# Scores of two heads on 64 rows of the array each, three products a head, in an encoder's attention

## The chip, the cores and the metric

The kernel runs on one core of one Trainium2 chip. The core has TensorE (PE in the profile; its weight loads are listed apart as PEld), VectorE (DVE), ScalarE (ACT), GpSimd (POOL) and SyncE (SP), and 16 DMA engines. The metric is the device time of one execution in microseconds (us).

## The reference

Two layers of an encoder on 512 tokens of width 1024, in float32. Each layer is a feed-forward half-step, a mixer with three attention branches, and a second feed-forward half-step. The mixer, cut to what matters here:

```python
u = rmsnorm(h, mix_pre_g[l])
qa, ka, va, qb, kb, vb, qc, kc, vc, gl = jnp.split(u @ w_in[l], split_at, axis=-1)
oa = neighbourhood_attention(...)    # A: 8 heads of 64, 2-D window and a bias
ob = sliding_window_attention(...)   # B: 8 query heads on 2 key heads, rotary, |i-j| <= 128, a sink logit
oc = differential_attention(...)     # C: 4 heads with two softmax maps each, rotary, dense
yb = jnp.einsum('bsnc,ncd->bsnd', branches, w_branch[l])
merged = jnp.sum(gates * yb, axis=2)
h = h + rmsnorm(merged @ w_out[l], mix_post_g[l])
```

Scores are q.k over a head width of 64, for all three branches.

## The kernel before

Activations lie transposed: channels on the 128 partitions, 512 tokens along the free dimension. A block of 128 channels of q or k therefore holds two heads of 64, the one on partitions 0 to 63 and the other on 64 to 127. To get float32 accuracy from TensorE's one-pass float32r, each operand is split into a high part (rounded) and a low part (the rest); `split` does it with one ACT copy and one DVE subtraction. A dense product of a 128x128 weight block with 512 tokens is three matmuls (high.high, high.low, low.high; `mm3`, lines 298 to 300), and one block of projected channels (`dense1`) is 24 of them, accumulated in one PSUM bank with the tag "mm". "Dense" below means these matmuls.

PSUM has eight banks: four "mm", three "at" (scores, transposes and transposed operands), one "o".

Scores before: `stacks` writes, for each head, by DMA, a tile of 128 rows whose upper half is the high part and whose lower half is the low part (tile "st"), and for keys also the swapped one (tile "sw"). With rows stacked so, the product q.k with all four pairs of parts is two matmuls over 128 rows (lines 1337 and 1338 in A and B, 1475 and 1476 in C). A stack costs two transfers of 64 rows, on the SP queue. The queue also carries the rotary shuffles ("sh") and the bias tables of branch A ("braw").

A and B are worked off in units of two heads ("aa0" to "aa3", "ab0" to "ab3"), the heads one after the other in `softmax_pv`: for each of four query blocks of 128, scores over a window of 256 or 384 keys; DVE adds the bias and takes the row's extreme in one instruction (line 1341); ACT takes the exponent with the row sum (1350); DVE the reciprocal (1355) and the scaling (1357). Then, for each of four key blocks: PE transposes of the probabilities (1365), a split (324 on ACT, 325 on DVE), and two matmuls with the values into bank "o" (1368, 1369); at the end ACT copies half of "o" (1371) and DVE adds the halves (1372). C does the same with the whole 512 keys and two maps a head (lines 1475 to 1503).

The order in which the units are written is the table `ORDER`: "qa0" makes q, k, v of a unit, "aa0" attends, "ga", "ya" and so on are gates and branch products (dense work). This order is a priority only. The framework's scheduler sets the order of instructions on each engine: it takes written order as priority and moves an instruction forward where an earlier written one still waits for an operand or a buffer by its own estimate. Buffers come from tagged pools with a fixed number of slots (`ABUFS`, `PBUFS`), and a tile waits until a slot of its tag is free. What the scheduler has ordered is then fixed: each engine works through its own list in order.

Of the kernel before, what the change touches and what calls it, by code (L numbers as in the profile page):

```python
# [34 lines left out]
KP = KF - 2 * KS  # L35
HOLD_OUT = ("g", "g", "g", "g", "g", "tx", "tx", "pt")
# [73 lines left out]
def encoder_kernel(ctx: ExitStack, tc: tile.TileContext, order, xT, wts, cols, rows, rpb, consts, tables, out):  # L110
# [10 lines left out]
    ABUFS = {"f": {"t": 4, "x": 10}, "m": {"t": 5, "h": 4, "rr": 2, "tx": 5, "st": 16, "g": 10, "s": 2, "pt": 4}}  # L121
# [27 lines left out]
    def f(t):  # L149
        return t.bitcast(F32)  # L150
# [1148 lines left out]
    def stacks(x, both):  # L1299
        hi, lo = split(x, "tx")  # L1300
        res = []
        for s in range(2):
            own = slice(64 * s, 64 * s + 64)
            st = big("st", F32R, name="st")
            nc.sync.dma_start(f(st)[0:64], f(hi)[own])
            nc.sync.dma_start(f(st)[64:128], f(lo)[own])
            sw = None
            if both:
                sw = big("st", F32R, name="sw")
                nc.sync.dma_start(f(sw)[0:64], f(lo)[own])  # L1310
                nc.sync.dma_start(f(sw)[64:128], f(hi)[own])
            res.append((st, sw))
        return res

# [14 lines left out]
    def softmax_pv(sq, sk, vof, bias, scale, sink, odst, oview):  # L1329
        ss, nmx = [], small("nmx")  # L1330
        sall, at = big("s", shape=(P, NT * T), name="s"), 0
        for i in range(NT):
            j0, j1 = window(i)
            n = (j1 - j0) * P
            sp = bank("at")[:, :n]
            qs = sq[0][:, i * P : (i + 1) * P]
            PE.matmul(sp, qs, sk[0][:, j0 * P : j1 * P], start=True, stop=False)
            PE.matmul(sp, qs, sk[1][:, j0 * P : j1 * P], start=False, stop=True)
            s = sall[:, at : at + n]
            at += n  # L1340
            V.tensor_tensor_reduce(
                out=s, in0=sp, in1=bias(i), scale=-1.0, scalar=3e38, op0=ALU.add, op1=ALU.min,
                accum_out=nmx[:, i : i + 1],
            )
            ss.append(s)
# [41 lines left out]
    def mixer(l, op, first):  # L1387
# [42 lines left out]
        def qkv_a(q, k, v):  # L1430
            sq, sk = stacks(plain(q, True, 0.125), False), stacks(plain(k, True), True)
            return sq, sk, turn(plain(v, True), 2)
# [3 lines left out]
        def attn_a(p, sq, sk, vof):  # L1436
            o = big("t", name="o")
            for s in range(2):
                softmax_pv(
                    sq[s], sk[s], lambda j, s=s: vof(j, s), biases(2 * p + s), 1.0, None,  # L1440
                    perm(o[64 * s : 64 * s + 64, :]), natural,
                )
# [7 lines left out]
        def attn_b(p, sq, skb, vofb):  # L1450
            o = big("t", name="o")
            for s in range(2):
                hd = 2 * p + s
                kv = hd // 4
                softmax_pv(
                    sq[s], skb[kv], lambda j, kv=kv: vofb(j, kv), bias_b, 0.125,
                    (sink[:, l, hd : hd + 1], nsink[:, l, hd : hd + 1]),
                    o[64 * s : 64 * s + 64, :], lambda ap: ap,
                )
            OT["b", p] = split(o, "g")  # L1460
# [3 lines left out]
        def attn_c(sq, sk, v):  # L1464
            vh, vl = v
            aa = []
            sall = big("s", shape=(P, NT * T), name="s")
            for i in range(NT):
# [3 lines left out]
                for s in range(2):  # L1472
# [8 lines left out]
                    e = big("tx", name="e") if s else sall[:, i * T : (i + 1) * T]  # L1481
# [54 lines left out]
        def qkv_b(c):  # L1536
            return stacks(rope(dense1(w, l, c, X), cosR, sinR), c == KB)

        def qkv_c(hd):
            sq = stacks(rope(dense1(w, l, QC + hd, X), cosR, sinR), False)  # L1540
            sk = stacks(rope(dense1(w, l, KC + hd, X), cosR, sinR), True)
            return sq, sk, turn(plain(dense1(w, l, VC + hd, X), False), 1)
# [40 lines left out]
        for u in ORDER.split():  # L1583
# [4 lines left out]
        hN = [big("s", shape=(P, 2, 2, T), name="h") for _ in range(2)]  # L1588
# [5 lines left out]
            l, "mix_post_g", (1.0, 1.0), ("ffn2_pre_g", l), gains, lambda tb, n: hN[tb // 2][:, tb % 2, n, :],  # L1594
# [129 lines left out]
```

## Time and profile before

| | us |
|---|---|
| three runs | 2440.2, 2442.27 (median), 2444.3 |
| the profiled execution, its own time | 2441.57 |
| its span in the profile | 2439.8 |

| engine | busy us | share |
|---|---|---|
| PE | 2404.1 | 99% |
| PEld | 2111.5 | 87% |
| DVE | 1797.8 | 74% |
| ACT | 1347.5 | 55% |
| POOL | 192.1 | 8% |

Busy times of PE are of overlapping matmuls with modelled ends: one takes 0.39 us where the next starts 0.23 us after it. So the cost of a matmul in a row of others is read from the distance between starts. The two mixers' attention lies between about 389 and 770 us and between about 1597 and 1995 us of the span. Line numbers in the profile of before are those of the functions above.

### The profile page before, as it was taken

Reading aid. Unit: us, or ns where it says so; the run is one execution under the profiler, and the core shown is the slowest. Engines: PE = TensorE matmul, PEld = TensorE weight load, DVE = VectorE, ACT = ScalarE, POOL = GpSimd, SP = SyncE. Lnnn points to the kernel's source line nnn. Section 1 sums busy time; section 2 is a strip of 40 time slices with the busy share of each in tenths; the row PEclk is TensorE's granted clock in tenths of the full one; section 3 lists DMA queues with packets and bytes.
Section 4 is the critical chain, followed back from the end, with each engine's and each line's share of the span. In section 5 each row is a group of like instructions: output and inputs, shape, how many; then the busy total and the mean of one; then the engine's idle time right before and its main releaser. Section 6 shows DMA issues by size and latency. Waiting matters only on the chain. (4 is left out here: it accounts for less than half of the span.)

```text
span 2439.8 us, 37786 instructions
## 1 busy us (share of the span) xinstructions
PE 2404.1 (99%) x14298; PEld 2111.5 (87%) x14298; DVE 1797.8 (74%) x2943; ACT 1347.5 (55%) x2471; POOL 192.1 (8%) x192
## 2 busy tenths in 40 slices
PE   9999999999999999999999999999999999999998
PEld 8999888888877889998899998888877778899987
DVE  8887976857667467888878878776676764788786
ACT  6555655646555365555655555555465554555553
POOL 0111000000111100110001110000001111011100
PEclk9999999999999999999999999999999999999999
DMA  5566536445442334654435565373454333356642
GB/s 170 162 163 182 169 132 175 116 113 149 111 131 95 111 105 132 169 154 162 170 95 157 156 173 190 116 183 106 113 143 124 110 103 121 96 147 165 184 144 87
DMA packets 119190, 340.59 MB, mean 140 GB/s; under 512 B 15968, under 2 KB 22752, under 8 KB 118496
## 3 DMA queue, kind: packets, MB, share of 16 engines
q1 hardware_dynamic: 91344, 224.85, 29.9%
q10 hardware_dynamic: 22032, 79.78, 10.9%
q0 software_dynamic: 5632, 33.56, 6.8%
q8 instruction: 112, 1.84, 0.3%
q14 instruction: 70, 0.57, 0.1%
HBM read 285.16 MB, written 48.23 MB: 137 GB/s over the span
## 5 line engine op out<-in xcount | busy, mean ns | idle before, releaser
L298 PE MATMUL mm<-X,w 128*128 128x512 f32 (+1 forms) x1044 | 397.1, 380 | 2.2 <-ACT w L199 1.7
L299 PE MATMUL mm<-X,w 128*128 128x512 f32 (+1 forms) x1044 | 396.8, 380 | 0.7 <-DVE X L522 0.7
L300 PE MATMUL mm<-X,w 128*128 128x512 f32 (+1 forms) x1044 | 396.1, 380 | 0.0
L200 DVE TENSOR_TENSOR w<-wr,w 128x512 fp32r<-128x512 f32 x360 | 255.3, 714 | 168.2 <-ACT w L199 167.0
L199 ACT ACTIVATE w<-wr 128x512 fp32r<-128x512 f32 x360 | 223.4, 627 | 226.6 <-PE mm L300 184.3
L842 PE MATMUL mm<-ht,l 128*128 128x256 f32 x1120 | 316.5, 283 | 0.0
L842 PE MATMUL mm<-ht,h 128*128 128x256 f32 x1120 | 316.3, 282 | 0.0
L842 PE MATMUL mm<-lt,h 128*128 128x256 f32 x1120 | 315.6, 282 | 0.0
L298 PEld LDWEIGHTS mm<-X,w 128*128 128x128 f32 x1044 | 197.4, 189 | 34.0 <-ACT w L199 1.9
L299 PEld LDWEIGHTS mm<-X,w 128*128 128x128 f32 x1044 | 197.2, 189 | 32.2 <-DVE X L522 1.1
L300 PEld LDWEIGHTS mm<-X,w 128*128 128x128 f32 x1044 | 197.1, 189 | 31.4
L842 PEld LDWEIGHTS mm<-ht,l 128*128 128x128 f32 x1120 | 213.1, 190 | 0.0
L842 PEld LDWEIGHTS mm<-ht,h 128*128 128x128 f32 x1120 | 213.0, 190 | 0.0
L842 PEld LDWEIGHTS mm<-lt,h 128*128 128x128 f32 x1120 | 212.7, 190 | 0.0
L1082 PE MATMUL mm<-wh,f 128*128 128x512 f32 x640 | 200.3, 391 | 0.0
L842 PE MATMUL mm<-X,h 128*128 128x256 f32 x1120 | 200.3, 279 | 0.0
L842 PEld LDWEIGHTS mm<-X,h 128*128 128x128 f32 x1120 | 171.2, 189 | 0.3
L842 PE MATMUL mm<-X,l 128*128 128x256 f32 x560 | 155.4, 278 | 0.0
L1082 PEld LDWEIGHTS mm<-wh,f 128*128 128x128 f32 x640 | 120.3, 188 | 26.9
L702 DVE TENSOR_TENSOR l<-wr,h 128x1024 fp32r<-128x1024 f32 x70 | 85.7, 1224 | 78.5 <-PE mm L842 78.5
L1082 PE MATMUL mm<-wl,f 128*128 128x512 f32 x320 | 126.6, 396 | 3.1 <-DVE wl L959 3.1
L324 ACT ACTIVATE hi<-at 128x256 fp32r<-128x256 f32 (+2 forms) x168 | 77.2, 474 | 73.4 <-PE at L1365 37.9
(366 smaller groups left out, 5458.5 us busy)
## 6 DMA issues: line engine op xcount, KB each, us to landing
wr<-in_wts_dram SPq DMA_DIRECT2D x223, 512.0 KB, 4.7
wr<-in_wts_dram ACTq DMA_DIRECT2D x152, 512.0 KB, 3.6
sum<-in_wts_dram POOLq DMA_DIRECT2D x64, 512.0 KB, 5.5
st<-hi SPq DMA_DIRECT2D x84, 128.0 KB, 2.5
st<-lo SPq DMA_DIRECT2D x84, 128.0 KB, 3.4
ap<-in_wts_dram SPq DMA_DIRECT2D x20, 512.0 KB, 6.7
a<-kept SPq DMA_DIRECT2D x32, 256.0 KB, 5.9
ap<-sum SPq DMA_DIRECT2D x16, 512.0 KB, 4.7
```

The lines of the kernel that those rows point to most:

```text
L199: A.activation(hi, raw, AF.Copy)
L200: V.tensor_tensor(out=lo, in0=raw, in1=f(hi), op=ALU.subtract)
L298: PE.matmul(acc, w[0], x[0], start=start, stop=False)
L299: PE.matmul(acc, w[0], x[1], start=False, stop=False)
L300: PE.matmul(acc, w[1], x[0], start=False, stop=stop)
L324: A.activation(hi, src, AF.Copy)
L702: V.tensor_tensor(out=W[g]["l1"], in0=raws[g][0], in1=f(W[g]["h1"]), op=ALU.subtract)
L842: PE.matmul(acc, ws[i], xs[j], start=start and k == n == 0, stop=stop and k == HK - 1 and n == 2, skip_group_check=True,)
L1082: PE.matmul(acc, x[i], w[j], start=start and n == 0, stop=stop and n == 2, skip_group_check=True)
```

## The change

`stacks` goes. `parts` splits q and k in place, with no transfer; only the two key heads of B are copied by DMA, so that each lies on both halves of the partitions (`twice`). `scores` makes the scores of both heads of a unit (in C: of both maps of a head) for one query block: one bank "at" for the head on rows 0 to 63, one bank "mm" for the head on rows 64 to 127, and three matmuls of 64 rows a head, written alternately. `attend` makes the scores of both heads over all query blocks first, and then calls `softmax_pv` for the one head and for the other. The score tiles "s" become 1280 wide instead of 2048, with three slots instead of two, and two of them are needed by a unit instead of one a head; "tx" gets a sixth slot.

```diff
+SW = 10 * P
...
-    ABUFS = {... "m": {"t": 5, "h": 4, "rr": 2, "tx": 5, "st": 16, "g": 10, "s": 2, "pt": 4}}
+    ABUFS = {... "m": {"t": 5, "h": 4, "rr": 2, "tx": 6, "st": 16, "g": 10, "s": 3, "pt": 4}}
...
-    def stacks(x, both):
...
+    def parts(x, twice=False):
+        if not twice:
+            return split(x, "st")
+        own = split(x, "tx")
+        res = []
+        for s in range(2):
+            pair_ = [big("st", F32R, name="kv") for _ in own]
+            for dst, src in zip(pair_, own):
+                for at in range(2):
+                    nc.sync.dma_start(f(dst)[64 * at : 64 * at + 64], f(src)[64 * s : 64 * s + 64])
+            res.append(tuple(pair_))
+        return res
+
+    def scores(q, k, i, ks):
+        out = [bank(tag)[:, : ks.stop - ks.start] for tag in ("at", "mm")]
+        qs = slice(i * P, (i + 1) * P)
+        for n, (x, y) in enumerate(((0, 0), (0, 1), (1, 0))):
+            for s in range(2):
+                own = slice(64 * s, 64 * s + 64)
+                PE.matmul(out[s], q[x][own, qs], k[y][own, ks], start=n == 0, stop=n == 2)
+        return out
...
-    def softmax_pv(sq, sk, vof, bias, scale, sink, odst, oview):
-        ss, nmx = [], small("nmx")
-        sall, at = big("s", shape=(P, NT * T), name="s"), 0
+    def attend(q, k, vof, bias, scale, sinks, odst, oview):
+        ss, nmx = [[], []], [small("nmx") for _ in range(2)]
+        sall, at = [big("s", shape=(P, SW), name="s") for _ in range(2)], 0
         for i in range(NT):
             j0, j1 = window(i)
             n = (j1 - j0) * P
-            sp = bank("at")[:, :n]
-            qs = sq[0][:, i * P : (i + 1) * P]
-            PE.matmul(sp, qs, sk[0][:, j0 * P : j1 * P], start=True, stop=False)
-            PE.matmul(sp, qs, sk[1][:, j0 * P : j1 * P], start=False, stop=True)
...
+            for s, sp in enumerate(scores(q, k, i, slice(j0 * P, j1 * P))):
+                ss[s].append(sall[s][:, at : at + n])
+                V.tensor_tensor_reduce(
+                    out=ss[s][i], in0=sp, in1=bias[s](i), scale=-1.0, scalar=3e38, op0=ALU.add, op1=ALU.min,
+                    accum_out=nmx[s][:, i : i + 1],
+                )
             at += n
...
+        for s in range(2):
+            softmax_pv(ss[s], nmx[s], lambda j, s=s: vof(j, s), scale, sinks and sinks[s], odst[s], oview)
+
+    def softmax_pv(ss, nmx, vof, scale, sink, odst, oview):
...
         def attn_c(q, k, v):
...
-                for s in range(2):
-                    sp = bank("at")
-                    qs = sq[s][0][:, i * P : (i + 1) * P]
-                    PE.matmul(sp, qs, sk[s][0], start=True, stop=False)
-                    PE.matmul(sp, qs, sk[s][1], start=False, stop=True)
+                for s, sp in enumerate(scores(q, k, i, WHOLE)):
...
```

`attn_a` and `attn_b` call `attend` once a unit, and the handover at the mixer's end takes the three "s" tiles and two "tx" tiles in place of two large "s" tiles.

The written order within a unit changes with it, and the scheduler makes another order of it. Three places of PE's list show how; line 1320 of the changed kernel is the matmul in `scores`, 1374 the transposes of probabilities, 1377 and 1378 the products with the values, 299 to 301 the dense matmuls. In the names, "at" and "mm" are banks, and numbers tell tiles apart.

First, the end of the scores of a head. On PE before, in the first unit of layer 0, the last scores of the first head (lines 1337, 1338) stand before dense matmuls; 20 of these follow until the first transpose:

```order
L1337 MATMUL at625_4169<-st584_4013,st579_4001 128x256
L1338 MATMUL at625_4169<-sw585_4016,st579_4001 128x256
L299 MATMUL mm718_4494<-X537_3645,w717_4479 128x512
L300 MATMUL mm718_4494<-X536_3644,w717_4479 128x512
L298 MATMUL mm718_4494<-X536_3644,w717_4479 128x512
L299 MATMUL mm718_4494<-X537_3645,w717_4479 128x512
L300 MATMUL mm718_4494<-X536_3644,w717_4479 128x512
```

On PE now, the scores of the first unit are followed at once by those of the second unit's head on rows 64 to 127 (banks mm665 to mm671, all four of the tag), and these by the transposes of the first unit's first head (s613), with no dense matmul between:

```order
L1320 MATMUL mm669_4316<-lo599_4095,hi595_4088 128x384
L1320 MATMUL mm669_4316<-hi598_4094,lo596_4089 128x384
L1320 MATMUL mm671_4326<-hi598_4094,hi595_4088 128x256
L1320 MATMUL mm671_4326<-lo599_4095,hi595_4088 128x256
L1320 MATMUL mm671_4326<-hi598_4094,lo596_4089 128x256
L1374 MATMUL at625_4181<-cons_66,s613_4128 128x128
L1374 MATMUL at628_4190<-cons_66,s613_4128 128x128
```

What moved: the dense matmuls that stood in the wait for the softmax stand later, and the three matmuls of a head's query block stand in a row on the same 64 rows.

Second, where dense work begins again. On PE now, the next dense matmul (mm702) stands behind the whole of both heads' products with the values (o639 is the second head's bank) and behind the scores of the second unit's other head (at664 to at670):

```order
L1320 MATMUL at664_4295<-hi598_4094,lo596_4089 128x256
L1378 MATMUL o639_4232<-lo651_4266,v585_4015 128x256
L1320 MATMUL at666_4305<-hi598_4094,hi595_4088 128x384
L1320 MATMUL at666_4305<-lo599_4095,hi595_4088 128x384
L1320 MATMUL at666_4305<-hi598_4094,lo596_4089 128x384
L1320 MATMUL at668_4315<-hi598_4094,hi595_4088 128x384
L1320 MATMUL at668_4315<-lo599_4095,hi595_4088 128x384
L1320 MATMUL at668_4315<-hi598_4094,lo596_4089 128x384
L1320 MATMUL at670_4325<-hi598_4094,hi595_4088 128x256
L1320 MATMUL at670_4325<-lo599_4095,hi595_4088 128x256
L1320 MATMUL at670_4325<-hi598_4094,lo596_4089 128x256
L299 MATMUL mm702_4441<-X534_3642,w592_4056 128x512
```

On PE before, at the same place in the first head's products with the values, dense matmuls stand between them:

```order
L1369 MATMUL o627_4183<-lo630_4188,v590_4032 128x256
L1368 MATMUL o627_4183<-hi632_4197,v590_4032 128x384
L1365 MATMUL at637_4213<-cons_66,s621_4156 128x128 x2
L299 MATMUL mm722_4527<-X537_3645,w721_4512 128x512
L300 MATMUL mm722_4527<-X536_3644,w721_4512 128x512
L1369 MATMUL o627_4183<-lo633_4198,v590_4032 128x384
```

What moved: from the first scores of unit aa0 to mm702, PE's list now holds attention alone. The same stands at unit aa3 (written before aa2) and at unit ab3 (written before ab2), in both layers: six such stretches.

Third, branch C. On PE before, the scores of the first head of C stand in twos between dense matmuls:

```order
L1475 MATMUL at1260_6851<-st1225_6669,st1214_6615 128x512
L1476 MATMUL at1260_6851<-sw1226_6672,st1214_6615 128x512
L298 MATMUL mm1290_6963<-hi980_5659,w1249_6798 128x512
L299 MATMUL mm1290_6963<-lo981_5660,w1249_6798 128x512
L300 MATMUL mm1290_6963<-hi980_5659,w1249_6798 128x512
```

On PE now, all 24 stand together, most of them alternating between the halves (at and mm), and five dense matmuls later come the first transposes (line 1499):

```order
L1320 MATMUL at1222_6806<-lo1184_6610,hi1174_6561 128x512
L1320 MATMUL mm1223_6807<-lo1184_6610,hi1174_6561 128x512
L1320 MATMUL at1222_6806<-hi1183_6609,lo1175_6562 128x512
L1320 MATMUL mm1223_6807<-hi1183_6609,lo1175_6562 128x512
L1320 MATMUL at1227_6826<-hi1183_6609,hi1174_6561 128x512
L1320 MATMUL at1227_6826<-lo1184_6610,hi1174_6561 128x512
L1320 MATMUL mm1228_6827<-hi1183_6609,hi1174_6561 128x512
L1320 MATMUL mm1228_6827<-lo1184_6610,hi1174_6561 128x512
L1320 MATMUL at1227_6826<-hi1183_6609,lo1175_6562 128x512
L1320 MATMUL mm1228_6827<-hi1183_6609,lo1175_6562 128x512
L299 MATMUL mm1247_6904<-hi954_5621,w1205_6730 128x512
```

What moved: between the first score and the transposes of the last query block stand 32 dense matmuls now, and 44 before.

Over the whole list there are 576 score matmuls now and 384 before. They stand in 40 groups with nothing else between. Taken two at a time where neighbours lie on different halves, they make 178 pairs (44 of 256 columns, 48 of 384, 86 of 512) and 220 without a partner (100, 100 and 20).

More of the change, by code (lines that the diff above doesn't have):

```diff
@@ L1430, in qkv_a, with attn_a @@
         def qkv_a(q, k, v):
[L1431 to L1432 removed]
+            return parts(plain(q, True, 0.125)), parts(plain(k, True)), turn(plain(v, True), 2)
         oa = [sb.tile([P, 4, T], F32R, tag="X", name=nm("oa"), bufs=BUFS["X"]) for _ in range(2)]
[L1436 removed]
+        def attn_a(p, q, k, vof):
             o = big("t", name="o")
[L1438 to L1442 removed]
+            attend(
+                q, k, vof, [biases(2 * p + s) for s in range(2)], 1.0, None,
+                [perm(o[64 * s : 64 * s + 64, :]) for s in range(2)], natural,
+            )
             OT["a", p] = tuple(t[:, p, :] for t in oa)
@@ L1536, in qkv_b @@
         def qkv_b(c):
-            return stacks(rope(dense1(w, l, c, X), cosR, sinR), c == KB)
+            return parts(rope(dense1(w, l, c, X), cosR, sinR), c == KB)
         def qkv_c(hd):
-            sq = stacks(rope(dense1(w, l, QC + hd, X), cosR, sinR), False)
-            sk = stacks(rope(dense1(w, l, KC + hd, X), cosR, sinR), True)
-            return sq, sk, turn(plain(dense1(w, l, VC + hd, X), False), 1)
+            q, k = (parts(rope(dense1(w, l, c + hd, X), cosR, sinR)) for c in (QC, KC))
+            return q, k, turn(plain(dense1(w, l, VC + hd, X), False), 1)
         def finish_c(hd):
```

50 lines of the change are left out of this document (17 added, 33 removed).

## The prediction

> **What bounds the kernel now.** I read the page first (engines), then the stretches of the two mixers, then the groups of instructions by line for what PE waits for in the attention, then the timeline of PE, DVE and ACT in the first unit, from which the steps are priced.
>
> ```profile
> span 2439.8 us, 37786 instructions
> PE 2404.1 (99%) x14298; PEld 2111.5 (87%) x14298; DVE 1797.8 (74%) x2943; ACT 1347.5 (55%) x2471; POOL 192.1 (8%) x192
> ...
> 389.00:770.00 381.00, 372.79 (x1827) 304.04 (x1825) 267.09 (x640) 215.10 (x484) 30.52 (x21) 1.00 0.45 124
> 1597.00:1995.00 398.00, 389.90 (x1916) 317.51 (x1915) 276.82 (x656) 223.11 (x497) 30.91 (x21) 1.00 0.45 125
> ...
> L1365 PE MATMUL at<-cons,s 128*128 128x128 f32 x320 | 52.5, 277 | 1.2 <-DVE s L1357 1.0
> L1368 PE MATMUL o<-hi,v 128*128 128x256 f32 (+1 forms) x128 | 41.9, 327 | 0.8
> L1337 PE MATMUL at<-st,st 128*128 128x256 f32 (+1 forms) x128 | 41.3, 325 | 2.7 <-DVE nmx L1341 2.7
> L1369 PE MATMUL o<-lo,v 128*128 128x256 f32 (+1 forms) x128 | 40.6, 323 | 5.2 <-DVE lo L325 5.2
> ```
>
> In the two mixer rows the columns are the length, then busy time and count of PE, PEld, DVE, ACT and POOL, and the granted clock (1.00). PE is busy 373 of 381 us and 390 of 398 us: it bounds the mixers as it does the rest, and DVE and ACT have room on the mean. The last figures of the four groups are PE's idle time ahead of them: over both layers all softmax units of A and B cost it 2.7 + 1.2 + 0.8 + 5.2 = 9.9 us, little because dense matmuls stand in the waits. So the change is worth what it does to the sum of PE's work and PE's waits, and there is at most some 10 us of waits to win in A and B.
>
> The prices, from the first unit of layer 0. PE, by distance between starts:
>
> ```profile
> 390.37 0.29 PE L1338 MATMUL at<-sw,st 128*128 128x256 f32 x1
> 390.49 0.34 PE L1337 MATMUL at<-st,st 128*128 128x384 f32 x1
> 390.67 0.34 PE L1338 MATMUL at<-sw,st 128*128 128x384 f32 x1
> 390.84 0.39 PE L299 MATMUL mm<-X,w 128*128 128x512 f32 x1
> 391.07 0.40 PE L300 MATMUL mm<-X,w 128*128 128x512 f32 x1
> ...
> 398.59 0.39 PE L298 MATMUL mm<-X,w 128*128 128x512 f32 x1
> 400.43 0.39 PE L1337 MATMUL at<-st,st 128*128 128x256 f32 x1 [1.45 <-DVE nmx L1341]
> ...
> 405.35 1.04 PE L1365 MATMUL at<-cons,s 128*128 128x128 f32 x8
> ```
>
> A matmul of 256 columns takes 0.12, of 384 columns 0.175 (0.18 and 0.17), of 512 columns 0.23; a transpose (1.04 - 0.28) / 7 = 0.11. Each ends 0.16 after the next has started (0.39 - 0.23). DVE and ACT:
>
> ```profile
> 389.10 0.60 ACT L1425 ACTIVATE x<-mm 128x512 f32<-128x512 f32 x1 [2.09 <-PE mm L300]
> 402.86 0.60 ACT L1350 ACTIVATE s<-s,nmx 128x384 f32<-128x384 f32 x1
> 403.46 0.49 ACT L1350 ACTIVATE s<-s,nmx 128x256 f32<-128x256 f32 x1
> 403.95 1.14 ACT L199 ACTIVATE w<-wr 128x512 fp32r<-128x512 f32 x2
> ...
> 398.80 0.76 DVE L1410 TENSOR_TENSOR bedge<-braw,mask 128x256 f32<-128x256 f32 x2 [1.41 <-DMA braw<-in_rpb_dram]
> 399.95 0.42 DVE L1341 CUSTOM_DVE_ANT_0 s<-at,bedge 128x256 f32<-128x256 f32 x1
> 400.30 0.55 DVE L1341 CUSTOM_DVE_ANT_0 s<-at,bmid 128x384 f32<-128x384 f32 x1
> 400.77 0.55 DVE L1341 CUSTOM_DVE_ANT_0 s<-at,bmid 128x384 f32<-128x384 f32 x1
> 404.08 0.18 DVE L1355 RECIPROCAL l<-l 128x4 f32<-128x4 f32 x1 [0.66 <-ACT s L1350]
> 404.29 1.28 DVE L1357 TENSOR_SCALAR s<-s,l 128x256 f32<-128x256 f32 x4
> 407.79 0.42 DVE L325 TENSOR_TENSOR lo<-at,hi 128x256 fp32r<-128x256 f32 x1
> 408.12 0.55 DVE L1410 TENSOR_TENSOR bmid<-braw,mask 128x384 f32<-128x384 f32 x1
> 408.59 0.55 DVE L325 TENSOR_TENSOR lo<-at,hi 128x384 fp32r<-128x384 f32 x1
> 411.88 0.67 DVE L1372 TENSOR_TENSOR o<-o,ot 64x512 f32<-64x512 f32 x1
> ```
>
> From start to start: the instruction with the bias 0.35 (256) and 0.47 (384), the exponent 0.49 and 0.60, the reciprocal 0.20, four scalings 1.2 to 1.28, a low part 0.33 (256) and, with the same 0.55 duration as line 1341, 0.47 (384), the last addition 0.60.
>
> **The change, part by part.** *The products.* Before, 128 matmuls of 256 columns, 128 of 384, 128 of 512: 15.4 + 22.4 + 29.4 = 67.2 us. Now 178 pairs and 220 without a partner (the order). If the two of a pair run wholly side by side, a pair costs as one: 144 x 0.12 + 148 x 0.175 + 106 x 0.23 = 67.6 us; if not at all, 101.0 us. So even at its best the products gain nothing: what pairing saves, the third product and the unpaired matmuls take back. No row has a matmul on 64 rows, so both ends stay.
>
> The Trainium skill ("TensorE: Matmul & The Clock Gate", Part 3) says that matmuls on different row groups run at the same time, starting about 4 ns apart; by that the sum would be the lower end.
>
> *The stretches without dense matmuls.* Six times PE's list runs from the scores of one unit to the first dense matmul behind it with attention alone. What dense work covered before is open there, and the time is that of the chain over DVE, ACT and PE. I add it up for the second of layer 0 (unit aa3), from the last dense matmul. The turn of v is still to come: copy 0.2 + 0.6, four transposes 0.44, three products of 256 and their end 0.5: DVE starts at 1.8. Seven of its eight bias instructions and a low part of v, 3 x 0.35 + 4 x 0.47 + 0.35 = 3.3, to 5.1; ACT, which by its order makes seven exponents behind the first, ends these at 6.1; reciprocal, four scalings, to 7.6. First low part at 7.8 (its transposes and ACT's copy follow the scalings); four of them 1.6, among them a scaling 0.3 and 0.3 of waiting for an "at" bank, to 10.0; three scalings 0.95; the addition 0.6, to 11.6; again transposes and copy 0.4, four low parts 1.6, to 13.6; the last value product, nine scores 6 x 0.175 + 3 x 0.12 = 1.4: 15.0 us. DVE alone holds 10.4 us of this, so it can't be much shorter. The first stretch has a load of the exponent table and bias tables on DVE besides (0.35 to 0.47 each, five of them): 16.5. The third (branch B) starts sooner, at 0.5, but its exponents wait for all four maxima, because of the sink: 15.0. In all 46.5 us a layer. In that time PE does of other work 16 transposes and 16 value products, 1.8 + 2.4, three times, and two turns of v, 0.9: 13.4. So the scores of these six units cost 33.1 us of PE's time a layer. Before, they cost 6 x (8 x 0.12 + 8 x 0.175) = 14.2 and some 5 us of waits (half of 9.9), of which I leave 1.5 to the units that still have cover: 33.1 + 1.5 - 14.2 - 5 = 15.4 a layer, **31 us** in both. What is late next: the dense matmuls. They are not lost, but done behind the stretch, where nothing more is waiting for cover. Chains 10% shorter or longer make it 22 to 40.
>
> *Branch C.*
>
> ```profile
> 638.60:654.30 15.70, 12.31 (x45) 1.00 0.12 34
> ...
> 640.50 0.14 DVE L1478 TENSOR_SCALAR nm<-nm 128x1 f32<-128x1 f32 x1
> 640.56 0.68 DVE L1477 TENSOR_REDUCE nm<-at 128x1 f32<-128x512 f32 x1
> 641.16 0.14 DVE L1478 TENSOR_SCALAR nm<-nm 128x1 f32<-128x1 f32 x1
> 643.60 0.54 DVE L1487 TENSOR_SCALAR e<-e,lc,misc 128x512 f32<-128x512 f32 x1
> 644.05 0.21 DVE L1478 TENSOR_SCALAR nm<-nm 128x1 f32<-128x1 f32 x2
> 644.18 0.75 DVE L1490 SCALAR_TENSOR_TENSOR s<-s,lc,e 128x512 f32<-128x512 f32 x1
> 644.84 0.68 DVE L1477 TENSOR_REDUCE nm<-at 128x1 f32<-128x512 f32 x1
> ```
>
> The first row is the dense matmuls (bank mm) from the first scores of a head of C to the transposes of its last query block: about 44 in 15.7 us. DVE's chain now, to the same point, by its order: start 1.0, eight reductions of 0.60, eight small ones 0.06, four reciprocals 0.08, four times 0.45 and 0.66, two gates and a weight split 0.60 each: 1.0 + 4.8 + 0.5 + 0.3 + 1.8 + 2.6 + 1.8 = 12.8, with 1.3 for ACT between: 14.1. PE's list has 32 dense matmuls there, so it waits whether pairs overlap or not. The 12 others are done later: 14.1 + 12 x 0.23 - 15.7 = 1.1 us a head, **9 us** for eight (ends: 0 where ACT's share is hidden, 16).
>
> *The covered units of B* (ab0, ab1): 2.4 us of scores before; now 1.8 with overlap, but then the first transposes, 22 dense matmuls (5.0) later, wait for DVE and ACT at about 8: 1.2; without overlap 3.6. Loss 0.6 to 1.2 for each of four: **3 us** (ends -2 and 5).
>
> *Changing between 128 and 64 rows.* No row shows it. The nearest is the 0.16 by which a matmul ends after the next has started: waiting that out at each change outside the stretches (12 groups, 24 changes) is **4 us**; ends 0 and, for all 80, 13.
>
> The page "TensorEngine Tiling (Array Packing)" of the Trainium skill, section "Key Properties", says that a change of the tiling mode drains TensorE; by that the price is this one.
>
> *The transfers.* 240 on SP's queue become 16.
>
> ```profile
> st<-hi SPq DMA_DIRECT2D x84, 128.0 KB, 2.5
> ```
>
> They are hidden now but for the start: "braw", queued behind them, holds DVE up 1.41 us and PE 1.45 us. That wait is in the 5 us taken off. Split tiles, slots and handover issue the same work: nothing, hidden behind PE; only the slots matter, three "s" for the four that two units need, which is why the second unit's scores sit in all four "mm" banks and keep dense matmuls out.
>
> Sum: 31 + 9 + 3 + 4 = 47 on the execution's own 2441.6 (its span is 2439.8; the median of the runs, 2442.3, is 0.7 above): **2488 us**.
>
> **The rivals.** (a) *Weaker*: hops in the stretches overlap more than I let them and C loses nothing: 22 + 0 + 0 to 3: 2463 to 2477. For it: one ACT or DVE instruction off in each sum. (b) *Faster or equal*: the open chain is hidden anyhow. With the waits of A and B gone and overlap complete, 2441.6 - 9.9 + 0.4 = 2432. It decides at a stretch of 9 us (own work 4.6 and the scores 4.7); DVE's 10.4 us of work in it speak against it. (c) *The pairs don't do what they say, and worse*: each matmul on the other half waits for the end of the one before, 0.16 for each of the 356 in pairs, 57 us. Where DVE sets the time part of it is hidden: in C 24 x 0.39 = 9.4 for 5.5 us costs perhaps 3 a head, 22; in B 4 a unit, 18: 2441.6 + 47 + 40 = 2529. Nothing speaks for it but that no row shows such a matmul. Plain no overlap, 3 us more, lies within the forecast.
>
> **How the numbers follow.** Forecast 0.62, (a) 0.22, (c) 0.11, (b) 0.05. Bounds of the terms taken together: low 22 + 0 - 2 + 0 = 20, high 40 + 16 + 5 + 13 = 74: 2462 to 2515; this takes in (a) and leaves out (b) and (c). A run tells from no change what is over 0.2% (4.9 us) off: slower 0.95, within 0.02, faster 0.03.
>
> **What would show it.** In the profile after: PE's idle time ahead of the transposes and value products of A and B several times 9.9 us, put down to DVE; six holes of PE at aa0, aa3, ab3, between scores and the next dense matmul 14 to 17 us; score matmuls of 64 rows with starts a few ns apart in C if they overlap, 0.23 if not; DVE waiting for no "braw". It is wrong if stretches are under 12 us, or if alternating matmuls stand 0.39 apart.

## The result, and the profile after

The changed kernel takes 2503.6 us (median of 4 runs, 2502.0 to 2506.4) against 2443.3 us of the kernel before in the same session (median of 4): ratio 1.0249, 95% interval 1.0231 to 1.0266, so 60.3 us slower. The prediction was 2488 us, 2462 to 2515. Its direction holds and the time lies in its range; the loss was sized at 47 us.

The page of the changed kernel, span and engines:

```profile
span 2500.8 us, 37693 instructions
...
PE 2440.9 (98%) x14490; PEld 2126.1 (85%) x14490; DVE 1801.8 (72%) x2943; ACT 1348.4 (54%) x2471; POOL 193.0 (8%) x192
```

DVE and ACT do what they did (1797.8 and 1347.5 before). The span grew by 61 us, PE's busy time by 37; PE now leaves 60 us of its span idle, 36 before. The groups of PE's attention lines, with busy time, mean ns of one, idle time ahead and its releaser:

```profile
L1374 PE MATMUL at<-cons,s 128*128 128x128 f32 x320 | 58.1, 305 | 11.0 <-DVE s L1366 10.8
L1378 PE MATMUL o<-lo,v 128*128 128x256 f32 (+1 forms) x128 | 48.2, 377 | 3.3 <-DVE lo L326 3.2
L1377 PE MATMUL o<-hi,v 128*128 128x256 f32 (+1 forms) x128 | 47.6, 373 | 2.7 <-ACT hi L325 2.3
L1320 PE MATMUL at<-hi,hi 64*128 64x512 f32 (+2 forms) x64 | 26.0, 406 | 10.7 <-ACT s L1483 10.2 <-DVE nmx L1346 0.2
```

The transposes of the probabilities (1374) and the value products (1377, 1378) wait 17.0 us where they waited 7.2; the scores of C wait 10.2 us for ACT's exponent (1483). The means of 1374, 1377 and 1378 rose as well (277, 327 and 323 ns before), so idle time does not hold all of the loss. Distances between starts do. Added up over all of PE's matmuls from both traces, by the group that starts the distance:

| us from start to start | before | after | change |
|---|---|---|---|
| scores of A and B | 39.6 | 66.3 | +26.7 |
| scores of C | 30.5 | 43.0 | +12.5 |
| value products of A and B | 41.5 | 59.2 | +17.7 |
| transposes of probabilities, A and B | 33.2 | 41.3 | +8.1 |
| dense of the projections, gates, branches | 1059.7 | 1053.0 | -6.7 |

That is 58.3 of the 61.0 us. The six stretches, each from the start of the last dense matmul to the start of the next; columns are the length, busy time and count of PE, PEld, DVE, ACT and POOL, then PE's granted clock:

```profile
388.94:409.38 20.44, 18.33 (x90) 14.10 (x88) 16.38 (x52) 13.06 (x35) 0.00 (x0) 0.75 0.21 63
447.64:466.00 18.36, 16.31 (x91) 12.26 (x89) 13.37 (x44) 11.94 (x35) 0.00 (x0) 0.91 0.10 29
586.75:606.13 19.38, 15.22 (x86) 11.99 (x84) 14.28 (x48) 9.97 (x30) 0.00 (x0) 0.82 0.23 86
1627.52:1648.14 20.62, 18.40 (x90) 14.14 (x88) 16.23 (x52) 13.06 (x35) 0.00 (x0) 0.75 0.20 65
1686.41:1703.75 17.34, 15.38 (x91) 10.95 (x89) 13.31 (x44) 11.94 (x35) 0.00 (x0) 1.00 0.12 31
1825.35:1845.56 20.21, 15.43 (x86) 11.88 (x84) 15.10 (x50) 10.54 (x31) 0.00 (x0) 0.83 0.24 81
sum 116.35, PE 99.07 PEld 75.32 DVE 88.67 ACT 70.50 POOL 0.00; mean PE 16.51 PEld 12.55 DVE 14.78 ACT 11.75 POOL 0.00
```

They stand where the prediction put them, at aa0, aa3 and ab3 of both layers, but last 116 us for 93, and in five of the six the granted clock is below 1, which the prediction did not foresee. And do the pairs overlap? PE in the third stretch, six matmuls of 384 columns:

```profile
587.52 0.33 PE L1320 MATMUL at<-kv,hi 64*128 64x384 f32 x1
587.54 0.34 PE L1320 MATMUL mm<-kv,hi 64*128 64x384 f32 x1
587.70 0.33 PE L1320 MATMUL at<-kv,hi 64*128 64x384 f32 x1
587.71 0.33 PE L1320 MATMUL mm<-kv,hi 64*128 64x384 f32 x1
587.87 0.33 PE L1320 MATMUL at<-kv,lo 64*128 64x384 f32 x1
587.89 0.34 PE L1320 MATMUL mm<-kv,lo 64*128 64x384 f32 x1
```

The two halves start 0.01 to 0.02 us apart, and the next pair follows 0.17 to 0.18 later: a pair costs what one matmul costs. That settles rival (c). So the loss lies in what stands around the products, and three explanations were open: the order (dense matmuls kept out), the clock that falls, and the 64-row products themselves.

### The profile page after: what moved, and what is told of

Read it like the earlier page. It is cut to its first block, busy times and chain, and to the rows that moved or that the text cites. A ratio compares the mean times of both kernels' runs of the same rounds, so it can differ in the third digit from the quotient of the medians.

```text
span 2500.8 us, 37693 instructions
## 1 busy us (share of the span) xinstructions
PE 2440.9 (98%) x14490; PEld 2126.1 (85%) x14490; DVE 1801.8 (72%) x2943; ACT 1348.4 (54%) x2471; POOL 193.0 (8%) x192
## 3 DMA queue, kind: packets, MB, share of 16 engines
q1 hardware_dynamic: 73424, 195.47, 24.2%
## 5 line engine op out<-in xcount | busy, mean ns | idle before, releaser
L300 PEld LDWEIGHTS mm<-X,w 128*128 128x128 f32 x1044 | 196.7, 188 | 33.1 <-DVE X L523 1.1
L843 PE MATMUL at<-X,w 128*128 128x256 f32 x840 | 110.5, 281 | 0.0
```

The costliest lines, as they stand in the source:

```text
L300: PE.matmul(acc, w[0], x[1], start=False, stop=False)
L843: PE.matmul(acc, ws[i], xs[j], start=start and k == n == 0, stop=stop and k == HK - 1 and n == 2, skip_group_check=True,)
```

## The experiments

The ratio of each is against runs of the kernel before on the same chip (2440.7 to 2443.2 us), and the differences below are against those. With intervals of about 0.17% on each side, two differences can be told apart from some 6 us on.

**1. The order with the old products.**

```diff
-        for n, (x, y) in enumerate(((0, 0), (0, 1), (1, 0))):
+        for n in range(2):
             for s in range(2):
-                PE.matmul(out[s], q[x][own, qs], k[y][own, ks], start=n == 0, stop=n == 2)
+                PE.matmul(out[s], q[s][0][:, qs], k[s][n][:, ks], start=n == 0, stop=n == 1)
```

> Undoes the products alone: two products a head on 128 rows with stacked operands and their transfers, as in the kernel before; the written order (all scores of both heads of a unit first, in banks "at" and "mm") stays as in the changed kernel. Theory (order): the loss is the attention without dense matmuls in between, with the clock that falls in it; the stretches stay, 17 to 21 us each, and the kernel takes 2485 to 2500 us. Rival (products): the third product, the 64-row matmuls without a partner and the changes of mode are the loss; then it is back at 2440 to 2450 us.

Measured: 2542.3 us, ratio 1.0413 (1.0397 to 1.0428), 101 us slower. The rival is refuted: with the old products this order is 40 us worse than with the new ones. The theory's number is missed too, for a wait it had not counted:

```profile
L1322 PE MATMUL mm<-st,st 128*128 128x256 f32 (+2 forms) x96 | 38.5, 408 | 22.8 <-DMA st<-lo 13.8 <-DVE nmx L1348 4.3 <-ACT e L1485 3.5
```

With both heads' scores first, nothing covers the transfers of the second head's stack, and PE waits 13.8 us for them in this group. With the other three groups of scores it is some 18 us, of the 40; how the rest divides was not tried. So in this order the new products, without transfers, cost less than the old ones with them. What the new products cost in the old order is experiment 2.

**2. The products with the old order.**

```diff
+        for s in range(2):
+            ...
+                sp = bank("at")[:, :n]
+                for m, (x, y) in enumerate(((0, 0), (0, 1), (1, 0))):
+                    PE.matmul(sp, q[x][own, i * P : (i + 1) * P], k[y][own, j0 * P : j1 * P], ...)
...
+            softmax_pv(ss, nmx, ...)
```

> Undoes the order in branches A and B alone: the two heads of a unit come one after the other as before, each in banks "at", with three products on 64 rows that have no partner; no transfers for the queries, branch C as in the changed kernel. Theory (order): no stretches without dense matmuls and no half clock in A and B; what is left is the unpaired third product, 1.5 x 37.8 - 37.8 = 19 us, and branch C's loss of about 17 us, less some 5 of waits: 2465 to 2480 us. Rival (products): with no pair at all in A and B it is no better than the changed kernel, 2500 us or more.

Measured: 2512.4 us, ratio 1.0291 (1.0276 to 1.0307), 71 us slower; the theory is off by over 30 us, and the time is in the rival's range: without the new order the new products lose no less than with it. No stretch of the long kind is left in A and B (none over 4 us), yet the scores there cost 76.0 us from start to start. PE in the first unit:

```profile
395.13 0.39 PE L299 MATMUL mm<-X,w 128*128 128x512 f32 x1
395.45 0.38 PE L1348 MATMUL at<-hi,hi 64*128 64x256 f32 x1
395.67 0.28 PE L1348 MATMUL at<-lo,hi 64*128 64x256 f32 x1
395.79 0.28 PE L1348 MATMUL at<-hi,lo 64*128 64x256 f32 x1
395.99 0.50 PE L300 MATMUL mm<-X,w 128*128 128x512 f32 x1
```

From dense start to dense start 0.86: the dense matmul's own 0.23, three scores at 0.117, and 0.28 more. The first score comes 0.32 after the dense start, the second 0.22 after the first, and the dense one 0.20 after the last score. I had left this out of the expectation, though the prediction had a price for it (0.16 a change, two changes a group). Experiment 7 measures it.

**3. Both heads' scores in banks "at".**

```diff
-        out = [bank(tag)[:, : ks.stop - ks.start] for tag in ("at", "mm")]
+        out = [bank(tag)[:, : ks.stop - ks.start] for tag in ("at", "at")]
```

> One word changed: both heads' scores go to banks "at", none to "mm"; everything else as in the changed kernel. PE's list then has dense matmuls between the scores of a unit and its transposes again, in A, B and C. Theory (order): the four "mm" banks, taken by the scores of the next unit until DVE comes to them, keep the dense matmuls out; without that the stretches are gone, the pairs cost as one, and the time is 2436 to 2455 us. Rival (products or slots): the order of the heads or the products are the loss, whatever the banks: 2485 us or more. A third possibility: three "at" banks for scores, transposes and the turn of v are too few, and PE waits for DVE ahead of each score: 2455 to 2480.

Measured: 2480.8 us, ratio 1.0157 (1.0142 to 1.0173), 39.5 us slower; the time lies at the upper end of the third possibility (2480), but its reason is not seen. Only one group of scores has waits of over 1 us in all (2.0, for ACT), no stretch is over 4.2 us, and the clock stays at 1 until the last 8.6 us. But the dense matmuls now stand between the scores, and the list has the heads three by three:

```profile
394.69 0.50 PE L301 MATMUL mm<-X,w 128*128 128x512 f32 x1
395.12 0.39 PE L1320 MATMUL at<-hi,hi 64*128 64x256 f32 x1
395.35 0.27 PE L1320 MATMUL at<-lo,hi 64*128 64x256 f32 x1
395.46 0.28 PE L1320 MATMUL at<-hi,lo 64*128 64x256 f32 x1
395.67 0.50 PE L299 MATMUL mm<-X,w 128*128 128x512 f32 x1
```

Scores now stand in 102 groups between other work, in place of 40. All scores cost 100.4 us, as much as the prediction's end without overlap (101.0). The stretches were traded for changes of mode and products without a partner.

**4. The clock.**

```diff
         op = bank("o")
+        for _ in range(FILL if fill else 0):
+            PE.matmul(op, fill[0][0][:, :P], fill[1][0], start=True, stop=True, skip_group_check=True)
```

> Adds work: behind the scores of the first head of the units aa0, aa3 and ab3 of each layer stand 16 matmuls of 512 columns (16 x 0.23 = 3.7 us at full clock) into the output bank that is overwritten afterwards, 96 in all, 22 us of PE's time. Theory (clock): in the stretches the clock falls to half because PE idles, and transposes, value products and the scores at its end take twice as long; with PE kept busy the clock stays at 1 and the kernel takes 2485 to 2500 us in spite of the added work. Rival (chain alone): the chain over DVE and ACT sets the stretches whatever the clock; the added matmuls lie in the idle time or lengthen it: 2503 to 2520 us.

Measured: 2510.1 us, ratio 1.0281 (1.0264 to 1.0298), 6.5 us above the changed kernel by the medians, in the rival's range. The first three stretches:

```profile
388.66:409.49 20.83, 20.13 (x107) 14.23 (x105) 16.38 (x52) 13.07 (x36) 0.00 (x0) 1.00 0.17 58
447.75:468.20 20.45, 20.35 (x106) 14.43 (x104) 13.38 (x44) 12.00 (x34) 0.00 (x0) 1.00 0.09 27
588.66:607.71 19.05, 17.76 (x102) 13.12 (x101) 14.25 (x48) 10.03 (x30) 0.00 (x0) 1.00 0.23 85
```

The clock is back at 1.00 in all three, and they are no shorter (20.83, 20.45, 19.05 for 20.44, 18.36, 19.38). The third is the clean one, since there the added work hides in the wait for the exponents. The first transposes of the changed kernel, and of this one:

```profile
595.26 1.97 PE L1374 MATMUL at<-cons,s 128*128 128x128 f32 x8 [2.83 <-DVE s L1366]
```

```profile
597.17 0.44 PE L1380 MATMUL at<-cons,s 128*128 128x128 f32 x2 [0.67 <-DVE s L1370]
```

Both start 8.51 us after their stretch began (586.75 and 588.66). From there to the next dense matmul it is 10.87 us at a granted clock that falls to a half for 6.83 us, and 10.54 at full clock. In the first stretch, with 10.24 us of half clock, it is 12.9 and 11.8. So in these two the clock is worth 0.3 and 1.2 us, not the half of its half-clock time (3.4 and 5.1): the chain over DVE and ACT sets the length. The Trainium skill ("TensorE: Matmul & The Clock Gate", Part 1) gives windows of about 3.4 us after which an idle array falls to half clock, and the spells seen here, 3.41, 6.83 and 10.24 us, agree. Its section "HAM oscillation — how this bites in real kernels" counts such a spell's cost as half its length, by which an estimate for the 41 us of this kernel is some 20 us; here the measured 0.3 and 1.2 us decide against that.

**5. The order, with everything else kept.** PSUM slots of a tag go round in written order, so a dense block written behind two attention units takes its "mm" slot behind the second unit's scores.

```diff
-qa0 qa1 aa0 aa1 qa3 qa2 aa3 aa2 kb ga2 ga1 ga0 qb0 ga4 ga5 ga7 ya5 ga3
-ga6 ab0 qb1 ya1 ya2 ya6 ya7 ab1 qb3 qb2 ya3 ya0 ya4 ab3 ab2 qc1 qc0 gb4
+qa0 qa1 aa0 qa3 aa1 qa2 aa3 kb ga2 ga1 aa2 ga0 qb0 ga4 ga5 ga7 ya5 ga3
+ga6 ab0 qb1 ya1 ya2 ya6 ya7 ab1 qb3 qb2 ya3 ya0 ya4 ab3 qc1 qc0 ab2 gb4
```

> The changed kernel with six units of the table ORDER written elsewhere, so that a unit of q, k, v (dense matmuls) or of gates stands between any two of aa0, aa1, aa3, aa2 and between ab3 and ab2; nothing else is touched. The slots of "mm" go round in written order: a dense block written behind two units of attention has to wait for the second unit's scores to leave "mm", one written between them only for the first unit's. Theory (order): in PE's list the dense matmuls are back in the softmax waits of all sixteen units of A and B, the scores stay in one group of 24 that costs about 2.06 us where the kernel before paid 2.4 and some waits; so A and B no longer lose, what is left is branch C's 12 us and it takes 2440 to 2455 us. Rival (products and changes of mode): A and B still lose by what 64-row products cost, 2480 us or more.

Measured: 2466.5 us, ratio 1.0109 (1.0092 to 1.0126): 25.8 us slower than before, where the changed kernel was 60.3. Two lines of a table take 34.5 us of the loss away with no product touched. PE in the first unit:

```profile
393.64 0.27 PE L1320 MATMUL at<-hi,lo 64*128 64x256 f32 x1
393.84 0.50 PE L299 MATMUL mm<-X,w 128*128 128x512 f32 x1
...
397.83 0.39 PE L301 MATMUL mm<-X,w 128*128 128x512 f32 x1
398.06 0.38 PE L1374 MATMUL at<-cons,s 128*128 128x128 f32 x2
```

Eighteen dense matmuls stand again between the last score and the first transpose, and nothing waits here. The theory holds for the list: the long stretches are gone. It does not hold for the rest, that A and B no longer lose, and its number was 11 us short. The value products are back at 43.0 us, but the scores of A and B at 45.4 instead of 39.6: eight units alternate and cost 2.07 in one group (3.47 one after the other), the other eight, whose scores a turn of v cuts in two, about 3.6 each without the 0.6 of the turn. C keeps its 43.3.

**6. The same, with C's old scores.** The edit puts `stacks`, two products and banks "at" back in `qkv_c` and `attn_c`.

> As the reordered kernel, and branch C has its scores as before the change: two products on 128 rows with stacked operands and their transfers, both maps in banks "at". Theory (order): C's 12 us are C's own, from the four groups of 64-row matmuls in one row that wait for ACT to free a bank; without them 2425 to 2442 us, about equal to the kernel before or a little faster. Rival: C's loss is not of its scores but of what A and B push into its time; then no faster than the reordered kernel.

Measured: 2485.7 us, ratio 1.0186 (1.0170 to 1.0201), 45.0 us slower. The theory is missed; the rival's number holds (no faster than the reordered kernel), but for another reason than it gave. C's scores are at 30.5 us as before, but at ab3 a stretch of 16.7 us (18.8 in layer 1) opened, in which PE's list puts a turn of v that waits for ACT's copy:

```profile
L1342 PE MATMUL at<-cons,x 128*128 128x128 f32 x72 | 12.8, 305 | 24.1 <-ACT x L1450 24.1
```

It says nothing on C; experiments 11 and 12 try it cleanly.

**7. The price of changing rows.**

```diff
-            own = slice(64 * s, 64 * s + 64)
+            own = slice(0, P)
```

> As the per-head kernel (heads one after the other, three products each, no pairs), but in A and B the products run over all 128 rows instead of 64, in the same places of PE's list: the scores are then sums over both heads, and the output is not the attention's. Branch C stays on 64 rows. It tells what a change between 64 and 128 rows costs. Theory (changes): every group of 64-row matmuls between others costs 0.3 us more than its columns, 102 groups in A and B, so 2512 - 30 = 2475 to 2488 us. Rival: 64-row matmuls are slow by themselves or it is the third product alone, and 2505 to 2515 us.

Measured: 2483.1 us, ratio 1.0176 (1.0161 to 1.0191): 42.4 us above the kernel before, the per-head kernel 71.0, and inside the theory's range. The 28.6 us between them, over 102 groups, are 0.28 a group, the number read in experiment 2. The Trainium skill ("TensorEngine Tiling (Array Packing)", section "Key Properties") says that a change of tiling mode drains TensorE; this run agrees, and 0.14 a change is just under the 0.16 which the prediction took.

**8. Four "s" slots.**

```diff
-... "tx": 6, "st": 16, "g": 10, "s": 3, "pt": 4}}
+... "tx": 4, "st": 16, "g": 10, "s": 4, "pt": 4}}
...
-        ms, r = small("ms"), small("rs")
+        ms, r = small("ms", 4, 1), small("rs", 4, 2)
```

> The changed kernel with four slots of the score tiles "s" instead of three (space taken from the padding and from "tx"), as two units need. The prediction gave the three slots as the reason why the second unit's scores sit in all four "mm" banks. If so, the dense matmuls come back and the time falls to 2440 to 2470 us. Theory (order of the banks): the slots of "mm" decide, PE's list stays as it is, and the time stays within 0.3% of the changed kernel's 2503.6 us.

Measured: 2524.7 us, ratio 1.0345 (1.0330 to 1.0361). PE's list is the changed kernel's, instruction for instruction, and the stretches stay, the first three:

```profile
393.81:414.08 20.27, 17.64 (x90) 12.77 (x88) 16.28 (x52) 12.97 (x35) 0.00 (x0) 0.83 0.19 59
452.39:470.64 18.25, 16.34 (x91) 12.44 (x89) 13.47 (x44) 12.00 (x35) 0.00 (x0) 0.91 0.09 29
591.12:610.31 19.19, 15.04 (x87) 11.70 (x85) 14.26 (x48) 10.01 (x30) 0.00 (x0) 0.82 0.24 84
```

So the three slots are not the reason that the prediction took them for. The theory is right on the list, but not on the time, which is 21 us above the changed kernel. These 21 us lie outside the attention: the feed-forward products of line 843 take 704.4 us from start to start for 692.7, those of line 1083 452.9 for 444.5. To make room for the slot the kernel moves tiles in memory and takes slots from two small ones; why those matmuls get slower stays open.

**9. Strict alternation in the reordered kernel.**

```diff
+        with tc.manual_schedule(engines={PE.engine}):
             for n, (x, y) in enumerate(((0, 0), (0, 1), (1, 0))):
```

> The reordered kernel, and the six matmuls of a query block are held in written order on PE, so that the two heads alternate in every group (in the reordered kernel many stand three by three). Nothing else is touched. In the reordered kernel the eight covered groups with a turn of v inside or with blocks three by three cost 2.5 to 3.8 us in all (serial sum 3.47), the eight that alternate 2.07. Theory (pairs): alternation halves the products, all sixteen units come to about 2.06 us, A and B gain 8 to 12 us: 2453 to 2460. Rival: pairing plays no part where dense work covers; 2463 to 2469 us.

Measured: 2472.3 us, ratio 1.0123 (1.0107 to 1.0138), 30.8 us slower: not better than the reordered kernel, and above both ranges. The scores of A and B fall to 39.6 us, 5.8 less, but the distances from a dense matmul to a turn of v grow from 2.3 us (10 of them) to 12.9 (18): with the group held together, the turn stands ahead of it and waits for ACT's copy.

```profile
389.71 0.39 PE L301 MATMUL mm<-X,w 128*128 128x512 f32 x1
390.79 0.66 PE L1327 MATMUL at<-cons,x 128*128 128x128 f32 x4 [0.69 <-ACT x L1435]
391.37 0.38 PE L1321 MATMUL at<-hi,hi 64*128 64x256 f32 x1
```

These rows are of experiment 10, which has the same edit; the turn starts 1.08 after the dense matmul, in place of 0.23. What the groups gained, the wait took.

**10. C's scores in banks "at" alone, on top of 9.**

```diff
-                for s, sp in enumerate(scores(q, k, i, WHOLE)):
+                for s, sp in enumerate(scores(q, k, i, WHOLE, ("at", "at"))):
```

> As the kernel with the matmuls held in order, and in branch C both maps' scores go to banks "at" (none to "mm"), so that PE's list has dense matmuls between the four groups of a head instead of 24 score matmuls in a row. Theory (banks): the holes of 4.5 to 6.5 us in C go; its 32 groups cost 3 x 0.23 + 0.3 = 0.99 each, 32 us for 43, and the time is 10 to 13 us below the kernel with matmuls held in order: 2440 to 2448, about equal to the kernel before. Rival: C's wait for ACT only moves to another place; within 4 us of the kernel with the matmuls held in order.

Measured: 2468.1 us, ratio 1.0105 (1.0088 to 1.0122), 4.3 us below experiment 9, less than can be told apart: nearer to the rival. C's scores fall from 43.4 to 35.2 us, but the distances from a dense matmul to a score grow from 5.1 us (16 of them) to 18.7 (46), with the changes and the waits for ACT that now stand there.

**11. The change in C alone.** A and B as in the kernel before; `parts`, `scores` and the new `attn_c` for C.

> The change in branch C alone: A and B, their order and their score tiles as in the kernel before, C with three products of 64 rows a map in banks "at" and "mm" and no stacks. The prediction gave C a loss of 9 us (0 to 16). Theory (C's own cost): its 24 score matmuls in a row wait for ACT's exponents to free bank "at", 5.4 us a head, 43 us in all for 30.5 before; the kernel takes 2450 to 2460 us. Rival: what C lost was due to A and B running into it; then 2438 to 2446 us.

Measured: 2459.0 us, ratio 1.0069 (1.0056 to 1.0081): 15.9 us slower. The theory holds. The wait is the changed kernel's:

```profile
L1335 PE MATMUL at<-hi,hi 64*128 64x512 f32 x32 | 14.1, 442 | 10.0 <-ACT s L1501 10.0
```

**12. The change in A and B alone, in an order with fewer holes.**

```diff
-... qb3 qb2 ya3 ya0 ya4 ab3 qc1 qc0 ab2 gb4
+... qb3 ya3 ab3 qb2 ya0 ya4 ab2 qc1 qc0 gb4
```

> The change in A and B alone, in an order without stretches: scores of A and B on 64 rows in pairs, written order as in the reordered kernel but with qb2 between ab3 and ab2 in place of qc1 and qc0, and C with two products of 128 rows and stacked operands as before the change. In the kernel that tried this with the other order a stretch of 16.7 and 18.8 us had come back at ab3, where the turn of v of C waited. Theory (order): that stretch goes, C's 12 us go, and what stays is the changes of mode and the products without a partner in A and B: 2446 to 2462 us. Rival: a loss as with the other order, 2475 to 2490 us.

Measured: 2467.3 us, ratio 1.0105 (1.0090 to 1.0121), 24.2 us slower, 5 us beyond the theory's range. The stretch at ab3 is gone, another has come behind ab1, in both layers:

```profile
561.38:570.27 8.89, 6.92 (x37) 4.65 (x35) 7.26 (x18) 3.63 (x7) 1.28 (x1) 0.73 0.32 98
1783.20:1792.26 9.06, 6.90 (x36) 4.65 (x34) 7.23 (x18) 3.63 (x7) 1.27 (x1) 0.74 0.31 94
```

Covered, a unit's scores pass in 2.3 to 4.5 us from dense matmul to dense matmul here, so the two holes are worth 9 to 13 us. No version tried beats the kernel before.

## Why the prediction was right, and where its terms were off

*The loss in parts.* Reordering takes off 34.5 us (60.3 - 25.8), the change in C alone costs 15.9, and 9.9 are left for A and B with all sixteen units covered. By experiment 12 that rest is 11 to 15 (24.2 less the two holes), so the parts do not add exactly; each carries some 6 us. Against the terms: stretches 31 forecast, 34.5 shown, measured against a kernel whose A and B, covered, still lose some 10; C 9 forecast, 15.9 shown; covered units and changes 3 + 4 forecast, for four covered units, 10 to 15 shown, for sixteen. The sum of 47 was short by 13, about half of it in C.

*The products.* The lower end (67.6 us) was right for matmuls that have work of the other half close by in the list; a head's three products alone between dense matmuls cost their serial sum (experiment 2). "Even at its best the products gain nothing" stands: the 39.6 us of experiment 9 are what A and B paid before. Experiment 1 adds what the prediction left out: within this order the new products save 40 us, some 18 of them waits for transfers.

*The stretches.* Their places were right, their length (14 to 17 us) was not. The step that failed is the end of the chain. From the second head's transposes to the next dense matmul the sum had 3.4 us (11.6 to 15.0, in the second stretch); the trace has 6.1 there (12.2 to 18.4) and 6.2 in the third (13.2 to 19.4). PE in the third:

```profile
599.93 1.03 PE L1374 MATMUL at<-cons,s 128*128 128x128 f32 x7
601.44 0.36 PE L1377 MATMUL o<-hi,v 128*128 128x256 f32 x1 [0.48 <-ACT hi L325]
...
603.00 0.50 PE L1320 MATMUL at<-kv,hi 64*128 64x256 f32 x2
603.43 0.44 PE L1378 MATMUL o<-lo,v 128*128 128x384 f32 x1
...
603.92 0.38 PE L1320 MATMUL at<-kv,lo 64*128 64x256 f32 x1
604.23 0.38 PE L1378 MATMUL o<-lo,v 128*128 128x256 f32 x1
604.54 0.61 PE L1320 MATMUL at<-kv,hi 64*128 64x384 f32 x2
```

PE waits for ACT's copy of the transposed probabilities, and then alternates value products on 128 rows with the second unit's scores on 64 rows, which have no partner left; the prediction charged changes "outside the stretches" only and 1.4 us for the last scores.

That the total came so near is in part luck. Added up from the trace, from start to start, the six stretches hold the scores of twelve units, 58.4 us, and the transposes and value products of six, 53.7. At the rates of the kernel before that would be 29.7 and 28.0. So the stretches cost 54 us more, where the sum had 38 (2 x (33.1 - 14.2)). On the other side the distances of dense matmuls fell by 6.7, and scores, transposes and value products outside the stretches cost no more than before (54.7 us for 56.6), where the sum had added 3 for covered units and a part of its 4 for changes. One small part is a miscount: the sum gave a unit 16 transposes, and the prediction's own row has 320 for 16 units, 20 each.

*The reason given for them* was wrong. Three "s" slots do not keep the dense matmuls out (experiment 8). The "mm" banks in their written order do: with no score in "mm" (experiment 3) or with dense work written between the units (experiment 5) the long stretches are gone.

*Branch C.* The step that failed took DVE's chain to the transposes for the limit. PE already waits inside the scores, for ACT: the fourth query block's scores need the "at" bank that the first block's exponent still reads, and that exponent started late, behind DVE's maximum. PE and ACT at a head of C in the changed kernel:

```profile
663.26 0.39 PE L1320 MATMUL mm<-hi,lo 64*128 64x512 f32 x1
664.07 0.69 ACT L1483 ACTIVATE s<-at,nm 128x512 f32<-128x512 f32 x1 [2.02 <-DVE nm L1479]
664.90 0.49 PE L1320 MATMUL at<-hi,hi 64*128 64x512 f32 x1 [1.25 <-ACT s L1483]
...
666.96 0.50 PE L299 MATMUL mm<-hi,w 128*128 128x512 f32 x1 [0.38 <-ACT e L1483]
```

The 24 scores of a head stand in a row in PE's list, so dense matmuls can't fill the wait: 15.9 / 8 = 2.0 us a head, 1.1 forecast.

*The changes of mode* were priced nearly right, 0.32 a group for 0.28, and charged too rarely: for the 12 groups outside the stretches (8 in C, 4 in covered units), where PE's list has 40, the other 28 of them in the stretches.

*The transfers.* PE's wait at the first unit is gone, as forecast. DVE's waiting for "braw" is not: 9.3 us after, 8.7 before, only earlier (the first at 376 us of the span, before at 399). So that sign was badly chosen. "PE idle several times 9.9" was another: 17.0 us ahead of transposes and value products, the rest of the loss being in longer distances.

*The rivals.* (a) and (b) fall with 60 us; the upper end of (a), 2477, does not follow from its own terms, which give 2467. (c) falls with the pairs' starts: no matmul waits for the end of the one on the other half.

## What to carry to other kernels

Before halving the rows of a product, count the places where its list changes between row modes: at 0.28 us a group a pair has to save more than that. In this kernel only the groups of 24 that alternate and have no other work between them came out below the price before (2.07 us for 2.4). When buffers of one tag go round in written order, a new user of the tag is also a new place in the queue for all others: look which block is written behind it, and move work between, before touching the arithmetic. And when a clock falls in a stretch, ask whether PE was what the stretch waited for; filling it with work brought the clock back and no time.

## What the runs showed of the hardware that was not expected

- A matmul on one half of the rows runs ahead of earlier listed ones on the other half. In the first unit the list has the three matmuls of a query block in bank "at" and behind them the last one of the same block's other head in "mm"; in the trace the "mm" one starts at 391.09, the three at 391.20, 391.38 and 391.55. So pairing does not need strict alternation in the list, only the other half's work close by.
- The granted clock fell to a half in spells of 3.41, 6.83 and 10.24 us, 41 us in all, and this cost 0.3 and 1.2 us in the two stretches where it was measured.
- With tiles moved in memory and small slots taken away (experiment 8), the feed-forward matmuls, which that edit does not touch, took 20 us more. Not explained.
